# First norm's shift and scale summed mostly on VectorE, all of the A projections beside them

## The chip, the cores and the metric

The kernel runs on one core of a Trainium2 chip. The metric is the device time of one execution in microseconds (us), and the lower the better. Before the change the median of three runs is 1560.95 us. All numbers are float32.

## What is computed

One residual block of a streaming encoder, for 256 tokens of width 2048. The reference, cut to what matters here:

```python
mod = silu(c) @ w_ada + b_ada                    # one row of 6 x 2048
sh1, sc1, gt1, sh2, sc2, gt2 = split(mod, 6)
h = rms_norm(x, g_mix) * (1 + sc1) + sh1
qa, ka, va, qb, kb, vb = split(h @ w_in, [1024, 256, 256, 1024, 1024, 1024])
o_a = band_attention_A(qa, ka, va)               # 16 heads, ALiBi and sinks
o_b = band_attention_B(qb, kb, vb)               # 16 heads, relative position bias
o = concat(rms_norm(o_a, g_out_a), rms_norm(o_b, g_out_b))
x = x + gt1 * (o @ w_out)
h = rms_norm(x, g_ffn) * (1 + sc2) + sh2
x = x + gt2 * hier_moe(h)                        # top-1 group of 4, top-2 experts of 8 in it
shf, scf = split(silu(c) @ w_ada_final + b_ada_final, 2)
y = rms_norm(x, g_final) * (1 + scf) + shf
```

Each of the conditioning rows (sh1, sc1, gt1 and so on) is a product of one vector of 2048 numbers with a matrix of 2048 columns: 16 MiB of weights are read for it, and each weight is used once. The products with `w_in` and `w_out` use each weight for 256 tokens.

## The kernel before, in words

All weights come through one **ring** of six slots of 2 MiB (class `Ring`, loads issued on SyncE's queue at L70 and L72). The order of the tiles in the ring is written out once, at the top of the kernel. A load is issued when the tile six places earlier has been released, and loads are issued strictly in this order. Each engine works through its own instructions strictly in the order of the code; a wait for another engine holds up all that stands behind it.

**First stage.** It runs over four quarters of the model width. For a quarter, four ring tiles (512 rows each) carry the columns of sh1 and sc1, and TensorE multiplies them with silu(c) (L297); the column `cact` holds silu(c), and four products of 32 rows each lie side by side in the array. The results are turned into columns (L313 to L320), applied to the turned and normalized x (`hT`, L324 and L326), and then the rows of `w_in` that belong to this quarter are multiplied: in 1024 columns, which are the second half of the A queries (`qA1`), the A keys and the A values (`kvA`), that is eight blocks of 128 columns (L332, L337). The first half of the A queries, `qA0`, waits for the next stage.

**Second stage**, with a loop over `order`. Each entry is one ring tile for TensorE, two to each block: `qA0`, `qB0`, `kB0`, `vB0`, `qB1`, `kB1`, `vB1` (`in_step`), and then eight tiles of `w_out` (`out_step`; the first four take the A half of the attention, the last four the B half). A tile of `in_step` is 32 products in two halves of 16 (`s` = 0 and 1); for the v blocks half as many of double width.

Between these tiles in the ring lie 44 **vector tiles** (`vec_tiles`) with the weights of gt1, sh2, sc2, gt2, scf and shf. VectorE multiplies them with silu(c) and adds them up over the rows (`vec_step`, four instructions on 128x1024 a tile, L360 and L365). Four tiles make one **sum** of 1024 columns, eleven sums in all. The table `VECTOR_TILES` says how many vector tiles follow each TensorE tile. The first of them is taken up by VectorE after the tile's first half, the others after its second half. When the fourth tile of a sum is done, `vec_finish` is put on the list `later`; the next call of `weave` runs it. It lets TensorE add up the 128 partitions (L378, "the close" of a sum below) and ScalarE copy the result. There is one accumulator: the first tile of the next sum stays in the queue until the close is in the code.

The attention is woven in as **rounds** of two heads (`weave(2)`): at the end of each `in_step` tile, and after each half of an `out_step` tile. In a round TensorE does the values of the heads two rounds back, turns those of the last round, and multiplies scores for two new heads; VectorE adds the bias, takes the maximum and, after ScalarE's exponentials, the reciprocals; GpSimd makes the A bias and scales. After the first half of an `in_step` tile `weave(0)` runs, which does only what is on `later`, the closes above all.

Behind that come the router and eight groups of experts, whose weights (w_gate, w_up, w_down) go through the same ring.

The first instructions load c, x and the small vectors on ScalarE's queue, in this order: c, x, the vectors of `pr` (biases and gains), the sinks, the router's weights, the relative bias. After them ScalarE computes the exponential for silu(c) at L243, and the squares of x at L273.

Of the kernel before, what the change touches and what calls it, by code (L numbers as in the profile page):

```python
# [38 lines left out]
VECTOR_TILES = [3, 0, 2, 2, 2, 2, 2, 2, 2, 2, 2, 4, 2, 3, 3, 2, 2, 2, 1, 2, 2, 0]  # L39
# [45 lines left out]
def block_kernel(ctx: ExitStack, tc: tile.TileContext, a: dict):  # L85
# [28 lines left out]
    blocks = [("qA0", 0), ("qB0", 1536), ("kB0", 2560), ("vB0", 3584), ("qB1", 2048), ("kB1", 3072), ("vB1", 4096)]  # L114
# [41 lines left out]
    x1 = keep.tile([128, 2, D], F32, name="x1")  # L156
    S.dma_start(out=x1, in_=a["x"].rearrange("(t p) n -> p t n", p=128))
# [7 lines left out]
    sinks = const.tile([128, NA], F32, name="sinks")  # L165
    S.dma_start(out=sinks, in_=a["sinks_a"].broadcast_to([128, NA]))
    wr = const.tile([128, 16, 36], F32, name="wr")
    br = const.tile([1, 36], F32, name="br")
    S.dma_start(out=br[:, 0:4], in_=a["b_router_group"])
    S.dma_start(out=br[:, 4:36], in_=a["b_router_expert"])  # L170
# [47 lines left out]
    with ExitStack() as sa:  # L218
# [6 lines left out]

        oT = pa.tile([128, 16, SEQ], F32, name="oT")
# [30 lines left out]

        gmix = pa.tile([128, 4, 4], F32, name="gmix")
# [30 lines left out]
        for q, (gemv, part) in enumerate(first_quarters):  # L289
            mods = [bank("s", f"shift{q}"), bank("s", f"scale{q}")]  # L290
            for s in range(2):
                PE.matmul(mods[s][0:32, :], lhsT=pick(ROW_ADA + 4 * s + q, 32), rhs=pr, start=True, stop=False, skip_group_check=True)
            for i, idx in enumerate(gemv):
                w = ring.get(idx)
                for s in range(2):
                    for k in range(4):
                        PE.matmul(  # L297
                            mods[s][32 * k : 32 * k + 32, :], lhsT=cact[:, 4 * i + k : 4 * i + k + 1].to_broadcast([128, 32]),
                            rhs=w[:, k, s, :], start=i == 0 and k > 0, stop=i == 3, skip_group_check=True,
                        )  # L300
                ring.release(idx)
            if q == 0:
                for k2 in range(8):
                    pt = bank("t", f"xt{k2}")
                    for kk in range(2):
                        for t in range(2):
                            c = 2 * k2 + kk
                            PE.transpose(pt[:, kk * 256 + t * 128 : kk * 256 + (t + 1) * 128], big[:, t, c * 128 : (c + 1) * 128], ident)
                    S.copy(hT[:, 2 * k2 : 2 * k2 + 2, :].rearrange("p k n -> p (k n)"), pt)
            cols = []  # L310
            for s in range(2):
                row = oT_flat[:, 2048 + s * 512 : 2048 + (s + 1) * 512]
                (S.copy if s else V.tensor_copy)(row, mods[s])  # L313
                pt = bank("t", f"mod{q}{s}")
                for c in range(4):
                    PE.transpose(pt[:, c * 128 : (c + 1) * 128], row[:, c * 128 : (c + 1) * 128], ident)
                col = small.tile([128, 4], F32, tag=f"mod{s}", name=f"mod{q}{s}")
                V.tensor_reduce(col, pt.rearrange("p (c r) -> p c r", c=4)[:, :, 0:128:32], axis=AX.X, op=ALU.add)
                cols.append(col)
# [162 lines left out]
        def values(kind, h):  # L482
# [12 lines left out]
            if h % 2:  # L495
# [9 lines left out]
                if h == (7 if kind == "A" else 15):  # L505
                    later.append([1, lambda: norm_o(kind)])
# [521 lines left out]
```

## Time and profile before

| what | us |
|---|---|
| median of three runs | 1560.95 |
| lowest, highest | 1560.94, 1568.42 |
| the profiled execution | 1562.42 |
| its span in the trace | 1560.7 |

The profiled execution is a run of its own beside the three. In the page of the profile TensorE (PE) is busy for 76% of the span, VectorE (DVE) 30%, ScalarE (ACT) 10%, GpSimd (POOL) 9%; the DMA engines moved 599.4 MB at a mean of 384 GB/s. These shares are means over stages that differ. The first stage runs to 137 us, the second to 548 us, of which the tiles of `w_out` begin at 397 us; the experts have the rest, from about 578 us on. The chain of work that ended last, as the page gives it, lies almost all in the experts' loads and products and begins only there, so the first two stages have to be read from the timelines of the engines. "PE" counts matmuls, "PEld" the weight loads that run beside them; a float32 matmul counts as two instructions, so a half of an `in_step` tile is x32. PEclk is the clock that TensorE was granted, as a share of 2.4 GHz.

### The profile page before, as it was taken

To read this page: it belongs to the slowest core of one execution; us is meant where nothing else is said; L and a number is where in the kernel's file an instruction comes from. 1 tells how busy PE (TensorE), PEld (TensorE's weight loads), DVE (VectorE), ACT (ScalarE), POOL (GpSimd) and SP (SyncE) were. 2 spreads that over 40 slices of the span, in tenths; PEclk is the share of its full clock that TensorE was granted. 3 is DMA by queue.
4 is the path that set the end of the run, shared out by engine and by line. 5 is a ranking of instruction groups with operands and counts; after the bars stand their busy time and mean duration, and the time that the engine had idled before them with its cause. 6 is when DMAs were issued, how large, how long until landed. Compare 5 with 4: busy or idle time off the path is not lost.

```text
span 1560.7 us, 14477 instructions
## 1 busy us (share of the span) xinstructions
PE 1181.1 (76%) x6073; PEld 533.7 (34%) x6074; DVE 462.6 (30%) x773; ACT 163.8 (10%) x420; POOL 142.7 (9%) x144
## 2 busy tenths in 40 slices
PE   4999999998989975765567577667657667567866
PEld 1657874873334541311211211211211121131211
DVE  1002667667697730220201201021021022022013
ACT  2101222131310110100100100100000010010001
POOL 0000433332332100000000000000000000000002
PEclk9999999998999988887788888878879888888889
DMA  9999999979799859799999999999999999999998
GB/s 353 390 392 389 352 335 363 373 292 382 300 379 399 332 224 422 313 385 411 422 402 422 421 392 422 421 389 421 421 412 421 421 394 421 422 390 421 421 388 333
DMA packets 128494, 599.40 MB, mean 384 GB/s; under 512 B 5832, under 2 KB 8440, under 8 KB 81064
## 3 DMA queue, kind: packets, MB, share of 16 engines
q1 hardware_dynamic: 124432, 593.51, 95.0%
q10 hardware_dynamic: 3960, 4.88, 0.9%
q8 instruction: 49, 0.80, 0.2%
q14 instruction: 21, 0.17, 0.0%
q0 software_dynamic: 32, 0.02, 0.0%
HBM read 596.02 MB, written 2.12 MB: 383 GB/s over the span
## 4 chain that ended last, share of the span: by engine, by line
DMA 34%; PE 16%; DVE 3%; ACT 1%; issue 0%; SPq 0%; DVEq 0%; ACTq 0%
DMA ring<-w_up 21%; DMA ring<-w_gate 9%; PE yp L795 5%; PE up L773 4%; DMA ring<-w_down 3%; PE gp L773 2%; PE g_g L737 2%; DMA ring<-w_ada_final 1%; DVE act_g L782 1%; ACT xg_g L744 1%; DVE xg_g L746 1%; PE sc_g L811 0%; PE at_g L788 0%; DVE act_g L783 0%; DVE act_g L784 0%
## 5 line engine op out<-in xcount | busy, mean ns | idle before, releaser
L773 PE MATMUL up<-ring,xg_g 128*32 128x512 f32 x1024 | 198.1, 808 | 120.3 <-DMA ring<-w_up 120.3
L773 PE MATMUL gp<-ring,xg_g 128*32 128x512 f32 x1024 | 169.5, 731 | 72.5 <-DMA ring<-w_gate 66.3
L795 PE MATMUL yp<-ring,actT_g 128*32 128x512 f32 x1024 | 156.3, 742 | 53.2 <-DMA ring<-w_down 47.4
L746 DVE TENSOR_SCALAR xg_g<-g_g,gsc,sh2c 128x128 f32<-128x128 f32 x64 | 26.3, 410 | 428.5 <-PE g_g L737 411.5
L773 PEld LDWEIGHTS up<-ring,xg_g 128*32 128x32 f32 x1024 | 43.4, 139 | 266.1 <-DMA ring<-w_up 155.0
L582 PE MATMUL po<-ring,oT 128*128 128x512 f32 x256 | 115.6, 607 | 0.0
L773 PEld LDWEIGHTS gp<-ring,xg_g 128*32 128x32 f32 x1024 | 39.6, 128 | 189.6 <-DMA ring<-w_gate 92.3
L816 POOL TENSOR_TENSOR big<-x,gscf 128x512 f32<-128x512 f32 x8 | 10.0, 1278 | 983.9 <-DVE x L813 983.9
L795 PEld LDWEIGHTS yp<-ring,actT_g 128*32 128x32 f32 x1024 | 36.3, 130 | 167.5 <-issue 91.5
L813 DVE TENSOR_TENSOR x<-x,sc_g 128x512 f32<-128x512 f32 x64 | 44.0, 687 | 152.2 <-PE sc_g L811 152.2
L744 ACT ACTIVATE xg_g<-g_g,sh2c,gsc 128x128 f32<-128x128 f32 x64 | 29.3, 458 | 538.6 <-DVE xg_g L746 538.6
L804 DVE TENSOR_TENSOR ys_g<-yp,gt2bc 128x512 f32<-128x512 f32 x32 | 22.1, 692 | 195.0 <-PE yp L795 195.0
L365 DVE SCALAR_TENSOR_TENSOR acc_gt<-ring,cact,acc_gt 128x1024 f32<-128x1024 f32 x60 | 78.7, 1312 | 1.9
L582 PEld LDWEIGHTS po<-ring,oT 128*128 128x128 f32 x256 | 48.9, 195 | 61.1 <-issue 61.1
L737 PE MATMUL g_g<-pn_g,big 128*128 128x128 f32 x512 | 64.3, 286 | 2.9 <-DVE pn_g L729 1.3
L737 PEld LDWEIGHTS g_g<-pn_g,big 128*128 128x128 f32 x512 | 61.1, 199 | 11.9 <-issue 8.8
L811 PE MATMUL sc_g<-ys_g,smat_g 128*128 128x512 f32 x128 | 61.7, 617 | 0.0
L549 PE MATMUL pw_vB<-ring,hT 128*128 128x512 f32 x128 | 58.4, 614 | 1.5 <-DMA ring<-w_in 1.5
L553 PE MATMUL pw_kB<-hT,ring 128*128 128x256 f32 x256 | 56.6, 381 | 0.0
L553 PE MATMUL pw_qB<-hT,ring 128*128 128x256 f32 x256 | 56.5, 381 | 0.0
L553 PEld LDWEIGHTS pw_qB<-hT,ring 128*128 128x128 f32 x256 | 48.2, 190 | 7.7 <-issue 1.0
L553 PEld LDWEIGHTS pw_kB<-hT,ring 128*128 128x128 f32 x256 | 48.2, 190 | 7.7 <-issue 0.7
(331 smaller groups left out, 1122.6 us busy)
## 6 DMA issues: line engine op xcount, KB each, us to landing
ring<-w_gate SPq DMA_DIRECT2D x64, 2048.0 KB
ring<-w_up SPq DMA_DIRECT2D x64, 2048.0 KB, 20.1
ring<-w_down SPq DMA_DIRECT2D x64, 2048.0 KB, 20.3
ring<-w_ada SPq DMA_DIRECT2D x32, 2048.0 KB, 10.3
ring<-w_in SPq DMA_DIRECT2D x18, 2048.0 KB, 13.0
ring<-w_ada SPq DMA_DIRECT2D x32, 1024.0 KB, 13.8
ring<-w_ada_final SPq DMA_DIRECT2D x15, 2048.0 KB, 8.9
ring<-w_out SPq DMA_DIRECT2D x8, 2048.0 KB, 14.4
```

Source lines behind the costliest of these rows:

```text
L365: V.scalar_tensor_tensor(acc, w[:, kk, :], cact[:, c : c + 1], acc, op0=ALU.mult, op1=ALU.add)
L549: PE.matmul(b[s], lhsT=hT[:, kk, s * 128 : (s + 1) * 128], rhs=w[:, k, :], start=kk == 0, stop=kk == 15)
L553: PE.matmul(b[s][:, n * 256 : (n + 1) * 256], lhsT=w[:, k, c * 128 : (c + 1) * 128], rhs=hT[:, kk, :], start=kk == 0 and n == 0, stop=kk = ...
L582: PE.matmul(b, lhsT=oT[:, (i // 4) * 8 + k, t * 128 : (t + 1) * 128], rhs=w[:, k, :], start=k == 0, stop=k == 7)
L737: PE.matmul(pm[:, i * 128 : (i + 1) * 128], lhsT=big[:, t, kk * 128 : (kk + 1) * 128], rhs=pn[:, t, :], start=t == 0 and i == 0, stop=t == ...
L744: S.activation(xg[:, kk, :], pm[:, i * 128 : (i + 1) * 128], AF.Identity, bias=sh2c[:, kk : kk + 1], scale=gsc2[:, kk : kk + 1])
L746: V.tensor_scalar(xg[:, kk, :], pm[:, i * 128 : (i + 1) * 128], gsc2[:, kk : kk + 1], sh2c[:, kk : kk + 1], op0=ALU.mult, op1=ALU.add)
L773: PE.matmul(bankt[32 * e : 32 * e + 32, :], lhsT=xg[:, kk, 32 * e : 32 * e + 32], rhs=w[e // 2][:, e % 2, j, :], start=kk == 0, stop=kk == ...
L795: PE.matmul(y[32 * e : 32 * e + 32, :], lhsT=aT[:, fc, 32 * e : 32 * e + 32], rhs=w(e)[:, n * 512 : (n + 1) * 512], start=fc == 0, stop=fc ...
L804: V.tensor_tensor(ys[:, n, :], yp[n], gt2bc[:, c : c + 512], op=ALU.mult)
L811: PE.matmul(pm, lhsT=sm[:, t * 128 : (t + 1) * 128], rhs=ys[:, n, :], start=True, stop=True)
L813: V.tensor_tensor(x1[:, t, c], x1[:, t, c], pm, op=ALU.add)
```

## The change

- **First stage.** In quarters 1 to 3 the first three of the four tiles with sh1 and sc1 go to VectorE (`acc_first`, twelve instructions on 128x1024 a quarter); the fourth goes to TensorE, with two products that add up VectorE's accumulator. Quarter 0 stays on TensorE. Shift and scale now share one PSUM bank and are turned together; the bias is added on VectorE (`bmod`) where TensorE did it before.
- The rows of `w_in` come as two tiles of 1.5 MiB a quarter (two times 128 rows of 1536 columns) for one of 2 MiB. They hold all of the A queries, keys and values: twelve blocks of 128 columns for eight.
- **Second stage.** `qA0` is gone: twenty tiles are left of 22. All sixteen A heads are ready at its start, and they run in the order 0 to 15; `VECTOR_TILES` has new numbers for the 44 vector tiles.
- **Start.** x, the sinks and the router's weights are loaded on ScalarE's queue behind the exponential for silu(c). x is turned after the second tile of quarter 0, not after the fourth.

```diff
-VECTOR_TILES = [3, 0, 2, 2, 2, 2, 2, 2, 2, 2, 2, 4, 2, 3, 3, 2, 2, 2, 1, 2, 2, 0]
+VECTOR_TILES = [3, 3, 2, 2, 2, 2, 2, 2, 2, 4, 2, 3, 3, 2, 2, 2, 2, 2, 2, 0]
...
-        first_quarters.append((gemv, ring.add((4, 1024), rows(w_in, q * 512, 4, 512, 1024))))
+        first_quarters.append((gemv, [ring.add((2, 1536), rows(w_in, q * 512 + h * 256, 2, 0, 1536)) for h in range(2)]))
...
-    blocks = [("qA0", 0), ("qB0", 1536), ("kB0", 2560), ("vB0", 3584), ("qB1", 2048), ("kB1", 3072), ("vB1", 4096)]
+    blocks = [("qB0", 1536), ("kB0", 2560), ("vB0", 3584), ("qB1", 2048), ("kB1", 3072), ("vB1", 4096)]
...
+            mods = bank("t", f"mods{q}")
+            on_vector = gemv[:3] if q else []
...
+                for k in range(4):
+                    c = cact[:, 4 * i + k : 4 * i + k + 1]
+                    if idx not in on_vector:
+                        for s in range(2):
+                            r = 64 * s + 32 * (k % 2)
+                            PE.matmul(
+                                mods[r : r + 32, :], lhsT=c.to_broadcast([128, 32]), rhs=w[:, k, s, :],
+                                start=i == len(on_vector) and k < 2, stop=i == 3 and k > 1 and not (q and k == 2), skip_group_check=True,
+                            )
+                    elif i or k:
+                        V.scalar_tensor_tensor(acc, w[:, k], c, acc, op0=ALU.mult, op1=ALU.add)
+                    else:
+                        V.tensor_scalar(acc, w[:, k], c, None, op0=ALU.mult)
+                ring.release(idx)
+                if q == 0 and i == 1:
+                    turn_x()
...
+            if q:
                 for s in range(2):
+                    PE.matmul(mods[64 * s : 64 * s + 32, :], lhsT=ones[:, 0:32], rhs=acc[:, s], start=False, stop=True, skip_group_check=True)
...
             for c in range(4):
                 kk = 4 * q + c
-                for n in range(6):
+                w = ring.get(parts[c // 2])[:, c % 2, :]
+                for n in range(10):
...
-        ready += [("A", h) for h in range(8, 16)]
+        ready += [("A", h) for h in range(16)]
...
-                if name == "qA0":
-                    ready += [("A", h) for h in range(8)]
```

How this moves instructions is seen at three places. Names are as in the code, with buffer numbers; ISA is an attention instruction with bias and maximum, and x4 are the four instructions of one vector tile.

VectorE at the start of the second stage, from the last reciprocal of the first round on. Before:

```order
L468 RECIPROCAL denA_746<-denA_746 128x2
L365 SCALAR_TENSOR_TENSOR acc_gt_696<-ring_577,cact,acc_gt_696 128x1024 x4
L365 SCALAR_TENSOR_TENSOR acc_gt_696<-ring_587,cact,acc_gt_696 128x1024 x4
L450 ISA stA_829,mxA_830<-spA_821,biasA_819 128x128
L450 ISA mxA_830 128x1
```

Now:

```order
L491 RECIPROCAL denA_758<-denA_758 128x2
L388 SCALAR_TENSOR_TENSOR acc_gt_708<-ring_584,cact,acc_gt_708 128x1024 x4
L388 SCALAR_TENSOR_TENSOR acc_gt_708<-ring_594,cact,acc_gt_708 128x1024 x4
L388 SCALAR_TENSOR_TENSOR acc_gt_708<-ring_662,cact,acc_gt_708 128x1024 x4
L473 ISA stA_853,mxA_854<-spA_845,biasA_843 128x128
```

All of the first sum's last three tiles stand between two rounds now; before, its last tile stood behind the second round.

VectorE between `kB1` and `vB1`, from the last reciprocal of the round on, with the second sum of sc2. Before:

```order
L468 RECIPROCAL denB_1915<-denB_1915 128x2
L365 SCALAR_TENSOR_TENSOR acc_sc_1823<-ring_1712,cact,acc_sc_1823 128x1024 x4
L365 SCALAR_TENSOR_TENSOR acc_sc_1823<-ring_1765,cact,acc_sc_1823 128x1024 x4
L360 TENSOR_SCALAR acc_gt_1950<-ring_1767,cact 128x1024
L365 SCALAR_TENSOR_TENSOR acc_gt_1950<-ring_1767,cact,acc_gt_1950 128x1024 x3
```

Now:

```order
L491 RECIPROCAL denB_1734<-denB_1734 128x2
L388 SCALAR_TENSOR_TENSOR acc_sc_1665<-ring_1523,cact,acc_sc_1665 128x1024 x4
L388 SCALAR_TENSOR_TENSOR acc_sc_1665<-ring_1582,cact,acc_sc_1665 128x1024 x4
L388 SCALAR_TENSOR_TENSOR acc_sc_1665<-ring_1584,cact,acc_sc_1665 128x1024 x4
L189 TENSOR_SCALAR rv_oA<-pnA 128x2
```

Three tiles of the sum stand behind that round for two. TensorE's close of this sum stands in both kernels after the first half of the first `vB1` tile.

VectorE in the tiles of `w_out`, with the end of the second sum of gt2; L586 and L609 are the step that takes a product's result. Before:

```order
L468 RECIPROCAL denB_2258<-denB_2258 128x2
L365 SCALAR_TENSOR_TENSOR acc_gt_2114<-ring_2056,cact,acc_gt_2114 128x1024 x4
L586 SCALAR_TENSOR_TENSOR hT<-po_2273,r_oA,hT 128x512
L360 TENSOR_SCALAR acc_scf_2309<-ring_2058,cact 128x1024
L365 SCALAR_TENSOR_TENSOR acc_scf_2309<-ring_2058,cact,acc_scf_2309 128x1024 x3
```

Now:

```order
L491 RECIPROCAL denB_2094<-denB_2094 128x2
L388 SCALAR_TENSOR_TENSOR acc_gt_2028<-ring_1889,cact,acc_gt_2028 128x1024 x4
L388 SCALAR_TENSOR_TENSOR acc_gt_2028<-ring_1891,cact,acc_gt_2028 128x1024 x4
L609 SCALAR_TENSOR_TENSOR hT<-po_2115,r_oA,hT 128x512
L473 ISA stB_2157,mxB_2158<-spB_2151,biasB_1846 128x128
```

The sum's third and fourth tile stand behind one round now; before, the fourth stood alone there. Its first and second tile stand behind the round before that one, where there was one tile before.

## Rows read from the trace of the kernel before

In the timelines a row is: start and duration in us, engine, line, operation, out<-in, shapes, count, and in brackets the idle time ahead of it with what ended it. Where a row merges several instructions its duration reaches to the end of the last.

**Rows 1.** Engines by stretch: start:end, length, busy us (instructions) of each; clock, DMA share, GB/s.

```profile
25.00:137.00 112.00, 104.35 (x591) 66.80 (x590) 11.22 (x32) 14.79 (x25) 0.54 (x1) 0.97 1.04 394
...
167.40:397.40 230.00, 216.75 (x989) 149.48 (x987) 154.55 (x269) 57.19 (x180) 76.46 (x74) 0.97 0.93 350
397.40:547.70 150.30, 141.65 (x435) 66.77 (x433) 114.88 (x138) 25.11 (x71) 43.25 (x32) 0.97 0.91 349
...
578.00:1560.70 982.70, 661.20 (x3732) 207.95 (x3732) 149.61 (x234) 52.64 (x113) 9.96 (x8) 0.85 0.98 405
```

**Rows 2.** Timeline of PE, first stage, quarters 1 and 3.

```profile
65.27 1.46 PE L316 MATMUL mod<-ident,oT 128*128 128x128 f32 x8
67.71 1.99 PE L332 MATMUL qA<-hT,ring 128*128 128x256 f32 x8 [0.99 <-DVE hT L326]
...
80.77 1.03 PE L337 MATMUL kvA<-ring,hT 128*128 128x256 f32 x4
...
107.31 1.04 PE L292 MATMUL shift<-pr,ident 128*32 128x512 f32 x2
...
116.05 0.66 PE L316 MATMUL mod<-ident,oT 128*128 128x128 f32 x4
...
120.08 3.75 PE L332 MATMUL qA<-hT,ring 128*128 128x256 f32 x8 [2.57 <-DMA ring<-w_in]
```

**Rows 3.** Timeline of PE, second stage: qA0's first tile, then blocks and a round.

```profile
137.02 14.06 PE L553 MATMUL pw_qA<-hT,ring 128*128 128x256 f32 x64
...
167.40 14.08 PE L553 MATMUL pw_qB<-hT,ring 128*128 128x256 f32 x64
...
199.74 0.66 PE L493 MATMUL opA<-ptA,big 128*64 128x256 f32 x4
...
202.22 14.08 PE L553 MATMUL pw_kB<-hT,ring 128*128 128x256 f32 x64
```

**Rows 4.** Waits of PE from 137 to 548 us: total us, times, longest.

```profile
PE pm_sc L378 <- DVE acc_sc L365: 8.0, 2, 6.2
...
PE pm_scf L378 <- DVE acc_scf L365: 3.1, 2, 2.4
PE pm_gt L378 <- DVE acc_gt L365: 2.9, 2, 1.7
PE pm_sh L378 <- DVE acc_sh L365: 2.5, 2, 1.3
```

**Rows 5.** Timeline of PE around two closes: sc2's second sum, gt2's second sum.

```profile
352.50 7.11 PE L549 MATMUL pw_vB<-ring,hT 128*128 128x512 f32 x16 [1.46 <-DMA ring<-w_in]
365.81 1.92 PE L378 MATMUL pm_sc<-acc_sc,ones 128*32 128x512 f32 x4 [6.21 <-DVE acc_sc L365]
367.67 9.28 PE L549 MATMUL pw_vB<-ring,hT 128*128 128x512 f32 x16
...
427.40 7.13 PE L582 MATMUL po<-ring,oT 128*128 128x512 f32 x16
436.26 1.05 PE L378 MATMUL pm_gt<-acc_gt,ones 128*32 128x512 f32 x4 [1.73 <-DVE acc_gt L365]
```

**Rows 6.** Timeline of DVE: a round's first instruction, and vector tiles behind rounds.

```profile
185.94 0.29 DVE L450 CUSTOM_DVE_ANT_0 stA<-spA,biasA 128x128 f32<-128x128 f32 x1 [9.09 <-PE spA L445]
...
206.76 10.69 DVE L365 SCALAR_TENSOR_TENSOR acc_gt<-ring,cact,acc_gt 128x1024 f32<-128x1024 f32 x8
...
355.04 10.72 DVE L365 SCALAR_TENSOR_TENSOR acc_sc<-ring,cact,acc_sc 128x1024 f32<-128x1024 f32 x8
...
430.65 5.56 DVE L365 SCALAR_TENSOR_TENSOR acc_gt<-ring,cact,acc_gt 128x1024 f32<-128x1024 f32 x4
```

**Rows 7.** Timeline of ACT at the start: a small load's issue, first square of x.

```profile
13.18 0.25 ACTq L164 DMA_DIRECT2D pr<-g_final  x1
...
22.92 1.90 ACT L273 ACTIVATE big<-x 128x2048 f32<-128x2048 f32 x1
```

**Rows 8.** Timeline of POOL: the last of the first four B biases.

```profile
152.60 0.20 POOL L429 MEMSET biasB<- 64x128 f32 x1 [2.00 <-DMA biasB<-scratch]
```

More of the change, by code (lines that the diff above doesn't have):

```diff
@@ L155, in block_kernel @@
     ring.pump()
-    x1 = keep.tile([128, 2, D], F32, name="x1")
-    S.dma_start(out=x1, in_=a["x"].rearrange("(t p) n -> p t n", p=128))
     pr = const.tile([128, 512], F32, name="pr")
@@ L164, in block_kernel @@
         S.dma_start(out=pr[row : row + n, :], in_=src.rearrange("o (r q) -> (o r) q", q=512))
[L165 to L170, printed above, removed]
     U = a["scratch"]
@@ L224, in bank @@
             return ps.tile([128, 512], F32, tag=tag, name=name, bufs=bufs)
+        pc = bank("m", "pc", 1)
+        PE.transpose(pc[:, 0:16], crow, ident[0:16, 0:16])
+        ce = pa.tile([128, 16], F32, name="ce")
+        S.activation(ce, pc[:, 0:16], AF.Exp, scale=-1.0)
+        V.tensor_scalar(ce, ce, 1.0, None, op0=ALU.add)
+        V.reciprocal(ce, ce)
+        V.tensor_tensor(cact, pc[:, 0:16], ce, op=ALU.mult)
+        x1 = keep.tile([128, 2, D], F32, name="x1")
+        S.dma_start(out=x1, in_=a["x"].rearrange("(t p) n -> p t n", p=128))
+        sinks = const.tile([128, NA], F32, name="sinks")
+        S.dma_start(out=sinks, in_=a["sinks_a"].broadcast_to([128, NA]))
+        wr = const.tile([128, 16, 36], F32, name="wr")
+        br = const.tile([1, 36], F32, name="br")
+        S.dma_start(out=br[:, 0:4], in_=a["b_router_group"])
+        S.dma_start(out=br[:, 4:36], in_=a["b_router_expert"])
         oT = pa.tile([128, 16, SEQ], F32, name="oT")
@@ L256, in columns @@
             return psum.rearrange("p (q r) -> p r q", q=4)[:, row : row + n, :]
+        bmod = pa.tile([128, 2, 4, 4], F32, name="bmod")
+        for s in range(2):
+            V.tensor_scalar(bmod[:, s], columns(p0, ROW_ADA + 4 * s, 4), float(s), None, op0=ALU.add)
         gmix = pa.tile([128, 4, 4], F32, name="gmix")
@@ L288, in block_kernel @@
         R["gt1"] = bflat[:, 3584:4096]
[L289 to L292, printed above, removed]
+        for q, (gemv, parts) in enumerate(first_quarters):
+            mods = bank("t", f"mods{q}")
+            on_vector = gemv[:3] if q else []
+            acc = pa.tile([128, 1024], F32, tag="acc", name=f"acc_first{q}").rearrange("p (s n) -> p s n", s=2) if q else None
@@ L293, in block_kernel @@
             for i, idx in enumerate(gemv):
                 w = ring.get(idx)
-                for s in range(2):
[L296 to L319, printed above, removed]
@@ new lines, in block_kernel @@
+            S.copy(row, mods)
+            pt = bank("t", f"mod{q}")
+            for c in range(4):
+                PE.transpose(pt[:, c * 128 : (c + 1) * 128], row[:, c * 128 : (c + 1) * 128], ident)
+            cols = small.tile([128, 2, 4], F32, tag="mod", name=f"mod{q}")
+            V.tensor_reduce(cols, pt.rearrange("p (c s h r) -> p s c h r", c=4, s=2, h=2)[:, :, :, :, 0], axis=AX.X, op=ALU.add)
+            V.tensor_tensor(cols, cols, bmod[:, :, q, :], op=ALU.add)
+            V.tensor_tensor(cols[:, 1, :], cols[:, 1, :], gmix[:, q, :], op=ALU.mult)
@@ L534, in weave @@
             del line[3:]
-        dest = {"qA0": (qA, 0.125), "qB0": (half["qB0"], 0.125), "qB1": (half["qB1"], 0.125), "kB0": (half["kB0"], 1.0), "kB1": (half["kB1"], 1.0)}
+        dest = {"qB0": (half["qB0"], 0.125), "qB1": (half["qB1"], 0.125), "kB0": (half["kB0"], 1.0), "kB1": (half["kB1"], 1.0)}
         open_banks = {}
```

54 lines of the change are left out of this document (30 added, 24 removed).

## Prediction

> **What bounds the kernel now.** First read the engines by stretch [rows 1]. In the first stage (25 to 137 us) the DMA share is 1.04 and TensorE is busy 104 of 112 us: loads set the pace and TensorE has little to spare. In the second stage it is the other way round: TensorE is busy 217 of 230 us and 142 of 150 us, the DMA share is 0.93 and 0.91. Whatever delays TensorE between 137 and 548 us delays the end, for behind it come the experts with a DMA share of 0.98 over 983 us [rows 1]; they start from a full ring in both kernels, so their length is the same and a shift of the second stage's end passes on in full.
>
> Then read TensorE's own waits in the second stage [rows 4]: nearly all are closes, that is TensorE waiting for VectorE to finish the last tile of a sum, 8.0 + 3.1 + 2.9 + 2.5 = 16.5 us. VectorE is busy only 155 of 230 us there [rows 1], so this is a matter of order, not of load. Between two rounds VectorE has its vector tiles; then it sits and waits for the scores, 9.09 us in one case [rows 6], with tiles already in the ring. It does not run ahead.
>
> **The first stage.** Its end before is 137.0, where qA0 starts [rows 3]. The last conditioning tile of quarter 3 landed one tile ahead of the `w_in` tile that TensorE waited for until 120.08 [rows 2]; 2.1 MB at 394 GB/s [rows 1] is 5.3 us, so at 114.8. The change adds 1 MiB of `w_in` to each of the three quarters before it, 3.1 MB or 8.0 us: 122.8. TensorE then does one tile's products (32 tiles' products and four bias products took from 107.31 to 116.05, 8.7 us for four tiles [rows 2], so 2.2), two products for VectorE's accumulator (0.5), and the vectors are turned to columns; that took 2.4 us between 65.27 and 67.71 [rows 2], and 3.0 with the copy now ahead of it. Block products start at 128.5; both `w_in` tiles have 3.1 MB to land by then or shortly after, and TensorE needs them one after the other. 32 products took from 67.71 to 81.8 [rows 2], 14.0, so 48 take 20.9: the stage ends at 149.4. A start at the lower clock costs more: after the wait of 2.57 us eight instructions took 3.75 us for 1.99, and the quarter ended at 137.0, 16.9 for 14.0 [rows 2]. That is 3 us, 152.4. I take 151.
>
> VectorE's twelve instructions a quarter cost nothing: three tiles by 5.35 us (half of 10.69 [rows 6]) are 16 us, it was busy 11 of 112 us there [rows 1], and it has the next quarter's tiles while TensorE does the block products. Without that cover each quarter would be up to 5 us longer. One bias product less, fewer turns and the two copies more behind the stage are under 1 us together and are left out; so is the earlier silu(c), since loads, not TensorE, set this stage's pace and the first release of a slot still comes before the six slots are full.
>
> x is issued behind the exponential and the small loads, at some 7 us by estimate, and six issues stand behind it on ScalarE before the squares. Before, x was issued second, an issue behind it was held until 13.18 and the first square stood at 22.92 [rows 7], held by these issues. The same chain now ends at 22 to 24 us, so quarter 0 starts its block products within some 2 us of before. The Trainium skill ("DMA: Bandwidth & Descriptors", Queues, rings and completion order) says that a DMA engine goes round the queues that have work, packet by packet, rather than first come, first served; by that x has half the rate and lands some 11 us after its issue, which fits the 13.18, and the late x below loses most of its chance.
>
> **What leaves the second stage.** qA0's two tiles are 2 x 14.06 = 28.1 us of TensorE [rows 3]. The two rounds between them do not vanish, they run later. So at equal waits the second stage's end shifts by 151.0 - 137.0 - 28.1 = -14.1 us.
>
> **What the new table does to the closes.** A close waits for VectorE's last tile. Three lengths, each with its rows: after TensorE leaves a round at 202.22 VectorE begins its tiles at 206.76, a lag of 4.5 for A heads; 4.0 for B heads in blocks (351.04, which is 352.50 less the DMA wait of 1.46, to 355.04); 3.2 in the tiles of `w_out` (427.40 to 430.65) [rows 3, 5, 6]. A vector tile takes 5.35, and 5.56 in `w_out` [rows 6]. TensorE takes 7.0 for half a block and 14.05 for a whole one [rows 3].
>
> So a close after the first half of the next tile, with n tiles of its sum behind the round, waits lag + 5.35 n - 7.0. Tried on before: sc2's second sum has n = 2, 4.0 + 10.7 - 7.0 = 7.7, less the 1.46 that TensorE had waited itself, is 6.2; measured 6.21 [rows 5]. gt2's second sum: 3.2 + 5.56 = 8.8, and 0.75 by estimate for the product's result, just in time for the next round; 9.6 + 3.2 + 5.56 = 18.4 against TensorE at 7.1 + 2.5 + 7.1 = 16.7 gives 1.7; measured 1.73. The 2.5 of a round is 199.74 to 202.22 [rows 3]. The formula holds on both.
>
> Now the eleven sums of the changed kernel, from the order of its instructions:
> - Sum 1 (gt1): three tiles behind the first round, close at the next tile's end. VectorE's part of that round waits for GpSimd, which does the first four B biases first, until 152.8, 15.8 after the stage began [rows 8]; with the lag of 4.5, VectorE is free at 20.3, and 0.2 more for the copies ahead. 20.5 + 16.05 = 36.5. TensorE is there after 14.05 + 0.9 (scores alone, a third of a round) + 14.05 = 29.0. Wait 7.5.
> - Sum 2: VectorE is still behind. From the close on: 3.5 (close, short round) + 4.5 + three tiles 16 = 24 against TensorE's next round ending at 3.5 + 14.05 + 2.5 = 20; VectorE's own part of it 3.5 (the lag without GpSimd's second), one tile: 32.9, against 27. Wait 5 to 6; I take 5.
> - Sums 3 to 5: n = 1 and a close after half a tile: 4.5 + 5.35 - 7.0 = 2.9, twice, and 2.4 with B heads. 8.2.
> - Sum 6 (sc2's second): n = 3. 4.0 + 16.05 - 7.0 = 13.0.
> - Sum 7: its close lies behind the spread of gate 1. 0.
> - Sum 8 (gt2's second): tiles one and two behind one round, three and four behind the next. 3.2 + 11.1 + 0.75 = 15.1, while TensorE's next round ended at 9.6; its own part some 2.9 (the lag less a start-up), then 11.1: 29.1, against 16.7. Wait 12.4.
> - Sums 9 to 11: rounds are over, one tile against half a step. 0.
>
> Together 46.1 for 16.5: +29.6. The bounds: with no lag at all each falls by its lag, to 16 together; with DMA waits and slower tiles on top 52. I take 46, since the formula met the waits of before.
>
> **Clock.** After the wait of 6.21 us the close took 1.92 for 1.05 and the next half block 9.28 for 7.11 [rows 5]: 3.1 us. Sum 6's wait had this before too, sum 1's is taken off sum 2's wait, sum 8's is new: +3.1, between 0 and 6. The Trainium skill ("TensorE: Matmul & The Clock Gate", What's actually happening) states that a slowed clock is the default and activity releases it; the row agrees. By that rule alone all three long waits would pay, +6.2 and 1582 in the end.
>
> **Sum.** The profiled execution took 1562.4, 1.5 over the median of the runs. 1562.4 - 14.1 + 29.6 + 3.1 = 1581.0; less 1.5 is 1579.
>
> **Rivals.**
> - *The closes hide: faster, 1547.* If VectorE took its tiles up while it waits for scores, the closes would cost 16.5 as before and -14.1 stands alone: 1546.8. For it: VectorE is idle a third of the stage [rows 1], and three closes of before wait for nothing. Against it: the idle 9.09 us and the order, in which tiles stand behind the round. It decides from where the waits and slow starts come to less than 16.5 + 14.1 = 30.6 together.
> - *The lags shrink by half: no change.* Waits near 31, no new slow start: 1562.4 - 14.1 + 14.6 - 1.5 = 1561. For it: ScalarE and GpSimd share in the lag and their load is laid out anew. Against it: all three measured lags lie between 3.2 and 4.5.
> - *x comes late: slower still, 1589.* If x moved only behind the six ring tiles, 12.6 MB or 32 us, it would land at 39; squares and scaling take some 9 and turning, two tiles and columns some 12 by estimate, so block products at 60 and the stage's end near 161 for 151. Against it: 13.18 [rows 7].
>
> **How the numbers follow.** The forecast 0.68, closes hidden 0.12, lags halved 0.12, late x 0.08. Some 0.5% (7.8 us) is what a measurement of this kernel can tell from no change. The first stage's end lies between 147 and 156 (-4, +5), the waits between 31 and 52 (-15, +6), the clock between 0 and 6 (3 either way). Range 1560 to 1593: it leaves out the faster rival and a part of the one beside it, and a little above. Faster by over 0.5% 0.12, within 0.5% 0.13 (part of the lags halved, and the low end of the forecast), slower 0.75.
>
> **What would show it.** Block products of quarter 3 end near 151. TensorE's waits for VectorE's sums total some 46 us, with three long ones: 7 to 8 at the end of the second qB0 tile, 13 in the first vB1 tile, 12 in the second tile of `w_out`. The second stage ends some 18 us later than before, the experts last as long. If these waits total under 30 us the prediction is wrong; if the first stage ends after 156 its sum is.

## The result: 1585.3 us, and the profile after

The changed kernel takes 1585.3 us in the median (1581.6 to 1585.8) against 1561.9 of the kernel before on the same chip: the ratio is 1.0136, with an interval of 1.0104 to 1.0168. It is slower by about 23 us, where 1579 was forecast and 1560 to 1593 was the range. The profiled execution took 1581.63 us, with a span of 1579.9.

First the engines by stretch, in the columns of [rows 1]: the first stage and the second, up to the end of the last product of `w_out`. First after, then before, whose second stage is cut here at the same event.

```profile
25.00:148.33 123.33, 109.94 (x527) 86.23 (x525) 54.94 (x66) 14.53 (x25) 2.21 (x4) 0.92 1.04 397
148.33:565.30 416.97, 365.58 (x1417) 217.03 (x1415) 284.40 (x429) 86.47 (x263) 124.53 (x117) 0.93 0.88 334
```

```profile
137.00:544.40 407.40, 385.59 (x1544) 239.16 (x1544) 285.75 (x431) 86.76 (x263) 127.79 (x117) 0.97 0.93 353
```

The first stage ends 11.3 us later. TensorE has 28.1 us less to do in the second stage, yet that stage is 9.6 us longer. Its idle time is 51.4 us (416.97 less 365.58) for 21.8: 29.6 more. Its busy time fell by only 20.0, so 8.1 us of the 28.1 came back as slower work; the clock column says 0.93 for 0.97. -28.1 + 29.6 + 8.1 = 9.6, and with 11.3 the second stage ends 20.9 us later. The experts, from their first product on, take 995.2 us after and 996.7 before.

The waits of PE in that stretch, as in [rows 4]:

```profile
PE pm_gt L401 <- DVE acc_gt L388: 25.4, 3, 11.8
PE pm_sc L401 <- DVE rv_oA L189: 12.7, 1, 12.7
PE pm_sh L401 <- DVE acc_sh L388: 5.6, 2, 2.9
PE pm_bc L426 <- ACT hT L427: 4.7, 3, 3.3
PE pm_sc L401 <- DVE acc_sc L388: 2.2, 1, 2.2
```

The closes are 46 of the 51 us. The second row names `rv_oA`, not the accumulator: that close also needs the PSUM bank that the norm of the A half holds, and VectorE reads it out right behind the three piled tiles. The timeline of DVE shows the pile (and below it the round's start at sum 1, with GpSimd's bias as releaser):

```profile
357.71 15.98 DVE L388 SCALAR_TENSOR_TENSOR acc_sc<-ring,cact,acc_sc 128x1024 f32<-128x1024 f32 x12
373.61 0.15 DVE L189 TENSOR_SCALAR rv_oA<-pnA 128x2 f32<-128x2 f32 x1
...
166.69 0.29 DVE L473 CUSTOM_DVE_ANT_0 stA<-spA,biasA 128x128 f32<-128x128 f32 x1 [12.84 <-POOL biasA L460]
...
170.19 15.98 DVE L388 SCALAR_TENSOR_TENSOR acc_gt<-ring,cact,acc_gt 128x1024 f32<-128x1024 f32 x12
```

And the timeline of PE at seven closes, to be held beside [rows 5]:

```profile
186.32 1.93 PE L401 MATMUL pm_gt<-acc_gt,ones 128*32 128x512 f32 x4 [9.14 <-DVE acc_gt L388]
188.00 1.96 PE L403 MATMUL pm_gt<-pr,ident 128*32 128x512 f32 x4
...
220.32 1.93 PE L401 MATMUL pm_gt<-acc_gt,ones 128*32 128x512 f32 x4 [4.48 <-DVE acc_gt L388]
...
223.88 7.88 PE L576 MATMUL pw_kB<-hT,ring 128*128 128x256 f32 x32
...
260.58 1.05 PE L401 MATMUL pm_sh<-acc_sh,ones 128*32 128x512 f32 x4 [2.87 <-DVE acc_sh L388]
261.56 7.13 PE L572 MATMUL pw_vB<-ring,hT 128*128 128x512 f32 x16
...
297.47 1.92 PE L401 MATMUL pm_sh<-acc_sh,ones 128*32 128x512 f32 x4 [2.71 <-DVE acc_sh L388]
299.32 7.70 PE L576 MATMUL pw_qB<-hT,ring 128*128 128x256 f32 x32
...
341.53 1.92 PE L401 MATMUL pm_sc<-acc_sc,ones 128*32 128x512 f32 x4 [2.18 <-DVE acc_sc L388]
343.38 7.87 PE L576 MATMUL pw_kB<-hT,ring 128*128 128x256 f32 x32
...
373.82 1.92 PE L401 MATMUL pm_sc<-acc_sc,ones 128*32 128x512 f32 x4 [12.70 <-DVE rv_oA L189]
375.67 8.74 PE L572 MATMUL pw_vB<-ring,hT 128*128 128x512 f32 x16
...
454.39 1.92 PE L401 MATMUL pm_gt<-acc_gt,ones 128*32 128x512 f32 x4 [11.76 <-DVE acc_gt L388]
```

Four instructions of a close take 1.05 us at the full clock and 1.92 at half of it. Before, one close took 1.92; now six of the seven with a wait over 1 us do, the one of 2.18 us among them. The 8.1 us came on top of the slow rows that the kernel before already had.

### The profile page after: what moved, and what is told of

It reads as the page before. It is cut to its first block, busy times and chain, and to the rows that moved or that the text cites. A ratio compares the mean times of both kernels' runs of the same rounds, so it can differ in the third digit from the quotient of the medians.

```text
span 1579.9 us, 14198 instructions
## 1 busy us (share of the span) xinstructions
PE 1170.6 (74%) x5909; PEld 529.9 (34%) x5910; DVE 505.2 (32%) x807; ACT 164.0 (10%) x420; POOL 139.8 (9%) x144
## 4 chain that ended last, share of the span: by engine, by line
DMA 34%; PE 16%; DVE 3%; ACT 1%; issue 0%; SPq 0%; DVEq 0%; ACTq 0%
DMA ring<-w_up 21%; DMA ring<-w_gate 9%; PE yp L816 5%; PE up L794 4%; DMA ring<-w_down 3%; PE gp L794 2%; PE g_g L758 2%; DVE act_g L803 1%; DMA ring<-w_ada_final 1%; ACT xg_g L765 1%; DVE xg_g L767 1%; PE sc_g L832 0%; PE at_g L809 0%; SPq L72 0%; DVE act_g L804 0%
## 5 line engine op out<-in xcount | busy, mean ns | idle before, releaser
L794 PE MATMUL gp<-ring,xg_g 128*32 128x512 f32 x1024 | 165.7, 716 | 70.8 <-DMA ring<-w_gate 64.9
L350 PE MATMUL qA<-hT,ring 128*128 128x256 f32 x256 | 61.6, 396 | 4.8 <-DVE hT L345 3.5
L576 PE MATMUL pw_kB<-hT,ring 128*128 128x256 f32 x256 | 60.2, 396 | 0.0
L350 PEld LDWEIGHTS qA<-hT,ring 128*128 128x128 f32 x256 | 50.6, 199 | 13.2 <-DVE hT L345 4.3
```

Source lines behind the costliest of these rows:

```text
L350: PE.matmul(early[n // 2][:, (n % 2) * 256 : (n % 2 + 1) * 256], lhsT=w[:, n * 128 : (n + 1) * 128], rhs=hT[:, kk, :], start=kk == 0 and n ...
L576: PE.matmul(b[s][:, n * 256 : (n + 1) * 256], lhsT=w[:, k, c * 128 : (c + 1) * 128], rhs=hT[:, kk, :], start=kk == 0 and n == 0, stop=kk = ...
L794: PE.matmul(bankt[32 * e : 32 * e + 32, :], lhsT=xg[:, kk, 32 * e : 32 * e + 32], rhs=w[e // 2][:, e % 2, j, :], start=kk == 0, stop=kk == ...
```

## The experiments

The theory: what the change gives (A's blocks in the shadow of the first stage's loads) is some 17 us, and the loss is made by the table, which puts the last tiles of a sum in piles behind a round; TensorE waits at the closes and starts slowly behind them. The rivals: the first stage with VectorE's new work, the later load of x, or the loads. In this table "ends" are the first stage's (start of the second stage's first block) and the second stage's (end of the last product of `w_out`), "busy" is TensorE's between them, all from the profiled execution; the ratio is to the kernel before on the same chip.

| kernel | median us | ratio (interval) | ends, us | busy |
|---|---|---|---|---|
| before | 1561.9 | 1 | 137.0, 544.4 | 385.6 |
| changed | 1585.3 | 1.0136 (1.0104 to 1.0168) | 148.3, 565.3 | 365.6 |
| a_table | 1541.8 | 0.9882 (0.9854 to 0.9911) | 148.2, 523.1 | 357.7 |
| b_table | 1588.5 | 1.0178 (1.0141 to 1.0214) | 134.7, 566.7 | 388.0 |
| a_late | 1563.5 | 1.0013 (0.9998 to 1.0029) | 148.0, 545.3 | 363.1 |
| a_tensor | 1588.8 | 1.0170 (1.0147 to 1.0193) | 155.1, 569.3 | 365.9 |
| a_best | 1539.6 | 0.9861 (0.9838 to 0.9884) | 147.8, 518.1 | 355.4 |
| b_best | 1544.8 | 0.9877 (0.9851 to 0.9903) | 136.8, 525.6 | 380.3 |
| a_again | 1583.4 | 1.0124 (1.0108 to 1.0140) | 148.6, 565.6 | 366.6 |
| a_dummy2 | 1573.8 | 1.0068 (1.0054 to 1.0082) | 150.1, 555.1 | 396.1 |
| a_xearly2 | 1581.8 | 1.0128 (1.0112 to 1.0144) | 146.9, 559.5 | 361.8 |
| a_best_x | 1539.5 | 0.9846 (0.9831 to 0.9862) | 147.0, 515.4 | 354.4 |

**Another table for the changed kernel.**

```diff
-VECTOR_TILES = [3, 3, 2, 2, 2, 2, 2, 2, 2, 4, 2, 3, 3, 2, 2, 2, 2, 2, 2, 0]
+VECTOR_TILES = [2, 1, 3, 1, 3, 1, 3, 1, 3, 4, 1, 5, 2, 3, 2, 2, 2, 2, 2, 1]
```

> The changed kernel with another table: the same 44 vector tiles in the same order beside the same twenty TensorE tiles, but divided [2, 1, 3, 1, 3, 1, 3, 1, 3, 4, 1, 5, 2, 3, 2, 2, 2, 2, 2, 1], so that the last tile of a sum mostly stands alone ahead of a round and not in a pile of two or three behind it. Theory (the waits at the closes, made by where the table puts a sum's last tile, are the loss, and the slow starts behind them come with them): TensorE's idle time of the second stage goes from 51.4 us to some 18 and its busy time from 365.6 to some 358; 1585.3 - 33 - 8 = about 1545, 1538 to 1555. Rival (the loss lies in the first stage, or VectorE's added work there, or in the ring): the waits come back at other closes or as waits for loads, 1575 to 1587.

1541.8 us, in the expected range and 43.5 us less than the changed kernel by one line of numbers. TensorE's first four closes, in its timeline, wait for nothing:

```profile
192.51 1.06 PE L401 MATMUL pm_gt<-acc_gt,ones 128*32 128x512 f32 x4
...
227.24 1.06 PE L401 MATMUL pm_gt<-acc_gt,ones 128*32 128x512 f32 x4
...
261.98 1.05 PE L401 MATMUL pm_sh<-acc_sh,ones 128*32 128x512 f32 x4
...
295.94 1.05 PE L401 MATMUL pm_sh<-acc_sh,ones 128*32 128x512 f32 x4
```

Idle time fell from 51.4 to 17.3 us (374.94 between the ends, less 357.65) and busy time by 7.9, both as expected. The first stage is untouched and ends when it did (148.2 for 148.3), so neither it nor VectorE's work in it is the loss.

**The piles in the kernel before.**

```diff
-VECTOR_TILES = [3, 0, 2, 2, 2, 2, 2, 2, 2, 2, 2, 4, 2, 3, 3, 2, 2, 2, 1, 2, 2, 0]
+VECTOR_TILES = [1, 1, 1, 3, 2, 2, 2, 2, 2, 2, 2, 4, 2, 3, 3, 2, 2, 2, 2, 2, 2, 0]
```

> The kernel before, with qA0 and its first stage as they were, but a table that makes the changed kernel's piles: [1, 1, 1, 3, 2, 2, 2, 2, 2, 2, 2, 4, 2, 3, 3, 2, 2, 2, 2, 2, 2, 0], the last eighteen numbers those of the changed kernel. Theory: closes wait by lag + 5.35 n - 7.0 as in the changed kernel, but for the first: about 4.5, 2.9, 2.6, 2.4, 13, 12, together some 38 for 16.5, +21, and slow starts of some 7 us more: 1561.9 + 28 = 1590, 1582 to 1598. Rival (the table isn't the cause): within 5 us of 1562.

1588.5 us, 26 more than before. The waits of PE from 137 us on:

```profile
PE pm_gt L378 <- DVE acc_gt L365: 17.4, 2, 11.7
PE pm_sc L378 <- DVE acc_sc L365: 16.6, 2, 13.1
PE pm_sh L378 <- DVE acc_sh L365: 5.0, 2, 2.9
...
PE pm_scf L378 <- DVE acc_scf L365: 0.8, 2, 0.6
```

39.8 us of closes where 38 were expected, with the long ones at the same sums. The table alone makes the loss, with or without qA0. Busy time rose by 2.4 us, less than the 7 that were expected of slow starts.

**A later close, the same table.**

```diff
-                later.append([1, lambda: vec_finish(name)])
+                later.append([2, lambda: vec_finish(name)])
```

> The changed kernel with its own table, but a sum's close is put on the list so that it runs at the second weave after the last tile, not at the next one: TensorE has 7 us more, or a round and a half tile, before it gets there. The first tile of the next sum starts later in turn, since there is one accumulator. Theory: sums 2 to 5 wait for nothing any more (-12 us), sums 1, 6 and 8 by some 7 us less each but for what the later start of the next sum gives back; idle from 51.4 to some 25 to 33, slow starts 4 us less: 1558 to 1570. Rival (VectorE is the limit there, and the closes only show it): the waits move to the next sums, over 1578.

1563.5 us. Idle time is 34.3 us, a little over what was expected; the waits of PE tell what stayed:

```profile
PE pm_sc L401 <- DVE rv_oA L189: 10.3, 1, 10.3
PE pm_bc L426 <- ACT hT L427: 8.2, 3, 6.9
PE pm_gt L401 <- DVE acc_gt L388: 7.4, 1, 7.4
PE pw_kB L576 <- DMA ring<-w_in: 5.3, 1, 5.3
```

Sums 1 to 5 are all but free (0.7 us), sums 6 and 8 are not, and the load of `kB0` is late. It was issued at 175.36, once VectorE had done the first of sum 1's three piled tiles and so given back its ring slot; in the changed kernel that load was issued as late (175.63), but there TensorE's wait at the close covered it. The waits didn't just move to the next sums, so VectorE's capacity isn't the limit.

**All of shift and scale on TensorE, twelve blocks kept.**

```diff
-            on_vector = gemv[:3] if q else []
+            on_vector = []
```

(with the accumulator and its two products taken out)

> The changed kernel with twelve blocks, but all sixteen tiles of sh1 and sc1 multiplied on TensorE as in quarter 0, none on VectorE. Theory (VectorE's part of the first stage is a gain and costs nothing): nine tiles by 2.2 us come back to TensorE, less three times two products, 18 us, against 13 us in which TensorE was idle there, most of it bound to turns and loads; a quarter then takes 20.9 + 8.7 + some 3 of turning, 32.6 for some 28: the first stage ends 8 to 15 us later than 148.3, and the time is 1593 to 1600. Rival (VectorE's tiles in the first stage hold up the stage, or push VectorE's work into the second): 1575 to 1585.

The first stage ends at 155.1, 6.8 us later, where 8 to 15 were expected. The last quarter in the timeline of PE:

```profile
124.58 7.07 PE L314 MATMUL mods<-ring,cact 128*32 128x512 f32 x64
132.41 0.66 PE L331 MATMUL mod<-ident,oT 128*128 128x128 f32 x4 [0.76 <-ACT oT L328]
134.25 3.72 PE L346 MATMUL qA<-hT,ring 128*128 128x256 f32 x16 [1.18 <-DVE hT L341]
```

Four tiles take 7.07 us here, not the 8.7 of [rows 2] with their bias products, and turning 2.6: 30.5 a quarter, not 32.6. The time is 1588.8 us, which misses the theory's 1593 to 1600 and the rival's 1575 to 1585 alike: in the median it is 3.5 us slower than the changed kernel, with intervals that overlap. VectorE's part is a gain at the stage's end and costs nothing that shows.

**Both cures, in the changed kernel and in the one before.** The later close, with a table for it: in the changed kernel

```diff
+VECTOR_TILES = [3, 2, 2, 3, 1, 3, 1, 3, 2, 2, 3, 3, 1, 3, 4, 2, 2, 2, 2, 0]
```

and in the kernel before

```diff
+VECTOR_TILES = [3, 2, 2, 2, 2, 1, 3, 2, 3, 2, 2, 2, 3, 2, 2, 2, 3, 0, 2, 1, 3, 0]
```

> The changed kernel with both cures together: the close at the second weave after the last tile, and the table [3, 2, 2, 3, 1, 3, 1, 3, 2, 2, 3, 3, 1, 3, 4, 2, 2, 2, 2, 0], laid out so that each sum has nearly a whole block between its last tile and its close. Theory (closes are the loss): idle of TensorE in the second stage some 12 us, most of it the spread of gate 1 and two late results, 1534, 1527 to 1541. Rival (after a_table something else sets the end, the ring or VectorE): 1541, as a_table.

> The kernel before with the same two cures: the close at the second weave, and a table for its 22 tiles, [3, 2, 2, 2, 2, 1, 3, 2, 3, 2, 2, 2, 3, 2, 2, 2, 3, 0, 2, 1, 3, 0]. It tells what the change itself is worth once closes cost neither kernel anything. Theory (the A blocks in the first stage are a gain of their own: 28.1 us leave the second stage, 11.3 come to the first): 16.8 us above a_best, less what of a_best's waits is left, so 7 to 17 above it: 1541 to 1551. Rival (the change gains nothing but room for a better table): within 4 us of a_best.

1539.6 and 1544.8 us. The first lies in the theory's range, but it can't be told from the rival's 1541 (a_table's interval overlaps), so nothing shows that the later close adds to a good table. The two are 5.2 apart in the median, between the theory's 7 to 17 and the rival's 4, and their intervals overlap. By the profiled executions the second stage ends 7.6 us earlier in a_best: it starts 11.0 us later (147.8 for 136.8) and lasts 18.5 less. Of the 28.1 us of qA0, then, 9.6 are lost again. The second stages, first of a_best, then of b_best:

```profile
147.78:518.05 370.27, 355.39 (x1414) 212.89 (x1412) 283.03 (x429) 85.65 (x262) 116.94 (x117) 0.98 0.96 370
```

```profile
136.83:525.64 388.81, 380.32 (x1542) 236.31 (x1541) 284.54 (x431) 85.95 (x262) 124.88 (x117) 0.99 0.96 365
```

Idle is 14.9 us for 8.5, busy 24.9 less and not 28.1. In a_best's waits a new row stands first:

```profile
PE po L605 <- DMA ring<-w_out: 5.8, 2, 5.2
```

So with the closes gone a load becomes the longest of TensorE's waits there. What the change is worth by itself is at best these 5 to 8 us, and the medians don't show that it is worth anything.

**TensorE kept at work while it waits.** Ahead of seven closes stand products that nobody reads:

```diff
+            for _ in range({("gt1", 0): 16, ("gt1", 2): 7, ("sh2", 0): 4, ("sh2", 2): 4, ("sc2", 0): 3, ("sc2", 2): 23, ("gt2", 2): 21}.get((name, lead), 0)):
+                PE.matmul(pm[32 * lead : 32 * lead + 32, :], lhsT=ones[:, 0:32], rhs=pr, start=True, stop=True)
```

> The changed kernel with its own table, and TensorE kept at work while it waits at closes: ahead of the products of seven sums stand 16, 7, 4, 4, 3, 23 and 21 products of ones with the vectors' tile, whose result is overwritten, 0.52 us each, a little less than each wait. No data move, and the close is due when it was. Theory (a close and the half tile behind it take longer only because TensorE had stood still before): the rows behind these closes go from 1.92 back to 1.05 us, TensorE's own work of the second stage from 365.6 to some 358, and the time falls by 5 to 8 us: 1577 to 1580. Rival (the slow rows have another cause, the load of the other engines or the total work): 1584 to 1588.

1607.9 us (ratio 1.0295, 1.0273 to 1.0317): the experiment was mis-sized. Its timeline of PE:

```profile
176.62 13.92 PE L400 MATMUL pm_gt<-pr,ones 128*32 128x512 f32 x32
...
371.39 20.84 PE L400 MATMUL pm_sc<-pr,ones 128*32 128x512 f32 x45 [12.70 <-DVE rv_oA L189]
...
460.47 17.78 PE L400 MATMUL pm_gt<-pr,ones 128*32 128x512 f32 x41
```

A product into the same 32 columns takes 0.87 us, not 0.52, and at sum 6 the filling itself waited for the bank and came on top. The three add 4.8 + 20.8 + 6.0 = 31.6 us, so this run's time decides nothing. With the right sizes, and a bank of their own:

```diff
+            count = {("gt1", 0): 10, ("gt1", 2): 5, ("sh2", 0): 2, ("sh2", 2): 2, ("sc2", 0): 2, ("sc2", 2): 14, ("gt2", 2): 13}.get((name, lead), 0)
+            if count:
+                idle = bank("t", f"idle_{name}{lead}")
+                for _ in range(count):
+                    PE.matmul(idle[0:32, :], lhsT=ones[:, 0:32], rhs=pr, start=True, stop=True)
```

> The changed kernel itself once more, beside the next two, so that differences of a few us can be read on one chip: 1585, 1582 to 1587.

> The filling of TensorE's waits again, now by the measured 0.87 us for such a product and into a bank of its own (the one before stood behind the bank that the sixth sum waits for, and added its 20.8 us to that wait): 10, 5, 2, 2, 2, 14 and 13 products, that is 8.7, 4.4, 1.7, 1.7, 1.7, 12.2 and 11.3 us, for waits of 9.1, 4.5, 2.9, 2.7, 2.2, 12.7 and 11.8. Theory (the slow rows behind a close come from TensorE's standing still, and cost some 8 us): the closes at 1.05 us, TensorE's span of the second stage 5 to 8 us shorter, 1577 to 1581 where the changed kernel has 1585. Rival (they cost nothing that the end sees, or have another cause): within 2 us of the changed kernel.

1573.8 us, 9.6 under the unchanged kernel beside it (1583.4), and the intervals of the ratios are apart. That is more than the theory's 5 to 8. Sums 1 and 2 in its timeline of PE:

```profile
178.92 8.77 PE L403 MATMUL idle_gt<-pr,ones 128*32 128x512 f32 x20
187.53 1.05 PE L406 MATMUL pm_gt<-acc_gt,ones 128*32 128x512 f32 x4
...
219.18 1.06 PE L406 MATMUL pm_gt<-acc_gt,ones 128*32 128x512 f32 x4
...
221.03 7.17 PE L581 MATMUL pw_kB<-hT,ring 128*128 128x256 f32 x32
```

Useless work made the kernel faster: closes take 1.05 us again and the half tile behind takes 7.17 for 7.88. The second stage is 12.1 us shorter (404.99 for 417.05). Of its busy time some 42 us are the useless products (48 by 0.87); without them it is 354 for the 366.6 beside it, 12 us less, so the gain is all in TensorE's own work, and waits and filling together last as long as the waits did (51 us for 50.5). From each of the six slow closes to TensorE's next row at full clock, the changed kernel takes 2.4, 2.4, 1.4, 1.6, 2.5 and 1.4 us longer than this one, 11.7 together. The theory's 8 was too small because it counted only the 8.1 on top of the kernel before, which had itself paid 3.0 at sum 6. The slow rows come from standing still. The Trainium skill ("TensorE: Matmul & The Clock Gate", What's actually happening) says that the slowed clock is the default and activity releases it; these rows agree.

**x loaded second again.**

```diff
     ring.pump()
+    x1 = keep.tile([128, 2, D], F32, name="x1")
+    S.dma_start(out=x1, in_=a["x"].rearrange("(t p) n -> p t n", p=128))
     pr = const.tile([128, 512], F32, name="pr")
```

(and taken out behind the exponential)

> The changed kernel with x loaded where it was before the change, second on ScalarE's queue, ahead of the small vectors; the turning of x stays behind the second tile. Theory (the first stage is paced by the loads, and x's place moves only its bytes): the first quarter's block products start some us earlier, but the stage ends at 148 within 2 us, and the time is 1585 within 3. Rival (x's later load holds up the first quarter and through it the stage): the stage ends 4 us or more earlier, 1577 to 1581.

> The changed kernel with x loaded second, as before, once more. Its first run was 7 us faster in the median, of which the trace showed 2 us at the end of the first stage. Theory (x later costs just what the first stage shows): 2 to 3 us under the changed kernel on the same chip. Rival (the place of x is worth more than the first stage shows): 5 us or more under it.

The first run gave 1578.3 us (ratio 1.0098, 1.0076 to 1.0121), below what the theory allowed and in the rival's range, though the first stage ends within the theory's 2 us of 148 and not 4 us earlier; the second gave 1581.8, 1.6 under the unchanged kernel on its chip, with ratios of 1.0128 and 1.0124. The total can't tell it from no change. The trace can at the stage's end: 146.4 and 146.9 for 148.3 and 148.6, some 2 us. Rows of the first of these runs, the last one of TensorE's weight loads (PEld):

```profile
40.70 3.69 PE L350 MATMUL qA<-hT,ring 128*128 128x256 f32 x16 [1.24 <-issue]
...
91.04 1.49 PE L315 MATMUL mods<-ring,cact 128*32 128x512 f32 x11 [1.61 <-DMA ring<-w_ada]
...
120.20 0.16 PEld L315 LDWEIGHTS mods<-ring,cact 128*32 128x32 f32 x8 [1.14 <-DMA ring<-w_ada]
```

Quarter 0 starts its blocks 3.6 us earlier than after the change (44.34), and about half is lost again to waits for loads. The last of them ends at 120.20, where the changed kernel has the same wait until 122.18 (its row is shown further down): with x earlier that load lands 2 us earlier.

**Everything together.** The later close and its table, with x second:

> The changed kernel with the later closes and their table, and x loaded second as before. Theory: the 1540 of the two cures less 2 to 3 of the first stage, as long as loads leave room: 1533 to 1539. Rival (with the closes gone the loads set the second stage, which already shows in a wait of 5.2 us for a tile of w_out): 1540, no gain from an earlier start.

1539.5 us, 1.5% under the kernel before and 2.8% under the changed one beside it in the medians. That is the rival's 1540 and just above the theory's range: an earlier x gives nothing that the median shows beyond a_best, though the second stage ends 2.7 us earlier. That loads take the rest back isn't shown; TensorE's waits for them there are 5.7 and 1.8 us, for 5.8 and 0.3 in a_best.

## Why the prediction was right, and where it wasn't

**The closes: right, sum by sum.** Forecast and measured waits in us:

| sum | 1 | 2 | 3 | 4 | 5 | 6 | 7 | 8 | 9 to 11 | all |
|---|---|---|---|---|---|---|---|---|---|---|
| forecast | 7.5 | 5 | 2.9 | 2.9 | 2.4 | 13.0 | 0 | 12.4 | 0 | 46.1 |
| measured | 9.1 | 4.5 | 2.9 | 2.7 | 2.2 | 12.7 | 0 | 11.8 | 0.9 | 46.7 |

The formula from three lags and one tile's length held on a new order. Sum 1 is 1.6 longer: GpSimd's last B bias was done 17.4 us after the stage's start, not 15.8 as in [rows 8]. The timeline of POOL after:

```profile
165.52 0.20 POOL L452 MEMSET biasB<- 64x128 f32 x1 [3.27 <-DMA biasB<-scratch]
```

All of TensorE's idle time grew by 29.6, the very number of the forecast; that it fits to a tenth is luck, since the single sums are off by up to 1.6. (The bound without lags comes to 18 by the prediction's own lengths, not 16; the 31 that rests on it would be 32.) Another table removed it (a_table), and the piles alone brought it to the other kernel (b_table).

**The clock: the step that failed.** The forecast took +3.1 us, from one new slow start, with 6 as its bound; the busy time shows +8.1. It read from [rows 5] that a wait of 6.21 is paid for and one of 1.73 is not, and let the waits of 2.2 to 5 us between them go free. The rows above show slow starts behind 2.18, 2.71 and 4.48: sums 5, 4 and 2, which cost 5.4 us together. The trace of before held a hint: behind its wait of 2.36 us the next 64 instructions took 29.30 us, where after the change they take 27.73. Sum 1's slow start, 2.4 us, was to come off sum 2's wait; that wait is only 0.5 shorter than forecast. Sum 8's, for which the 3.1 stood, cost 1.4. The prediction's sentence on the Trainium skill's rule, which made all three long waits pay (+6.2) and gave 1582, came nearer in size, but it too let sums 2, 4 and 5 go free. a_dummy2 shows that the cost is real: 9.6 us.

**The first stage: the reason right, the number 2.7 us too high.** 151 was forecast, 148.3 came. In the timeline of PE, quarters 2 and 3:

```profile
98.47 5.41 PE L350 MATMUL qA<-hT,ring 128*128 128x256 f32 x16 [1.18 <-DVE hT L345]
...
121.07 2.60 PE L315 MATMUL mods<-ring,cact 128*32 128x512 f32 x13
...
127.51 3.72 PE L350 MATMUL qA<-hT,ring 128*128 128x256 f32 x16 [1.18 <-DVE hT L345]
```

The same tile in the timelines of TensorE's weight loads (PEld), in the changed kernel and then in a_table, whose first stage is the same:

```profile
122.18 0.16 PEld L315 LDWEIGHTS mods<-ring,cact 128*32 128x32 f32 x8 [0.97 <-DMA ring<-w_ada]
```

```profile
122.04 0.16 PEld L315 LDWEIGHTS mods<-ring,cact 128*32 128x32 f32 x8 [1.16 <-DMA ring<-w_ada]
```

Quarter 3's blocks begin at 127.51 for 128.5 and take 20.8 for 20.9. The forecast had the last conditioning tile land at 122.8; its second half is waited for until 122.18, a wait that the row of PE hides in the 2.60 us of its thirteen instructions. So loads set the end of the stage, as forecast, but only by a little: TensorE had begun that tile at 121.07, and before it waited for no load from quarter 0's blocks on. In a_table quarter 0's blocks begin 1.8 us earlier (42.55 for 44.34) and the stage still ends at 148.2, with longer waits for loads. Of the 2.7 us, 1.0 lies in the landing and the turning, and 1.6 is the slow start, for which half of 3 us had been added. It came in quarters 0 and 2 (5.38 and 5.41 for 3.72), where it only shortens the wait for loads behind it (1.0 us in all, for 3.6 in a_table), and not in 3. That x's later load would let quarter 0 start within 2 us of before was right (44.34 for 42.51).

**qA0 and the experts: as forecast.** The 28.1 us left, and the experts took 995.2 for 996.7.

**The sum.** In the profiled execution 1581.0 was forecast: -2.7 in the first stage, 0 in the idle time, +5.0 in the clock, -1.7 from the end of the second stage to the end of the span make 1581.6, and it took 1581.63. The errors cancelled, which is luck: the clock was too low by 5.0, the first stage and the rest too high by 4.4. The median is 3.7 above that execution; the forecast had taken 1.5 off, because the profiled execution of before stood above its median. That was no property of the kernel.

**The rivals.** That the closes hide fell with 46.7 us of waits, that lags halve with the table above, the late x with 44.34. What the forecast of the faster rival, 1547, assumed (closes that cost no more than before) can be had by another order: a_table gives 1542.

## What to carry to other kernels

When an engine in the middle of a chain collects a sum for another one, put the sum's last piece alone and ahead of the work that can block it, or let the collecting instruction come a step later; work out every such meeting point by lag + pieces x length - cover before a table is changed, for here 44 tiles in another division were worth some 43 us. Count the slow clock with each such wait, short ones too: kept busy with useless products, TensorE won 9.6 us. And a gain moved from one stage to another is worth only what the next limit leaves: 16.8 us at the boundary (28.1 less 11.3) were at best 5 to 8 at the end.

## What the runs showed of the hardware

- How long TensorE waits doesn't tell alone whether it starts slowly: behind 2.18 us the close ran at half the clock (1.92 us), behind 2.87 at the full one (1.05). And behind the same wait of 1.18 us the blocks of quarter 2 started slowly (5.41 us), those of quarters 1 and 3 didn't (3.72). Which other thing decides stays open.
- Products into the same 32 columns one behind another took 0.87 us each; the two products of a close, which lie in two groups of columns, took 1.05 together.
- The first stage's end varied from 147.8 to 150.1 us between kernels whose first stages are the same (a_best, a_dummy2); the 150.1 has a slow start in quarter 3 (5.41 us for 3.72), which the others don't have. With x second it was 146.4, 146.9 and 147.0, earlier than in any of them, so the 2 us of x are small but show in three traces.
